# A decoder trunk's compressed-attention branch on one core: four heads in one score bank, one exponent and one sum for all heads, one reduction for the block importance, two heads per transpose

## The chip, the cores and the metric

The kernel runs on one core of one Trainium2 chip. The metric is the device time of one execution in microseconds (us), lower is better. A core has five engines with a queue of instructions each: TensorE (PE in the profile, its weight loads PEld), VectorE (DVE), ScalarE (ACT), GpSimd (POOL) and SyncE (SP, which issues most transfers). TensorE's granted clock is 1.00 when it runs at its upper level of 2.4 GHz.

## The reference, cut to what matters

The trunk has two layers on a stream of 1024 tokens of width 1024, all in float32. Layer A is a sparse attention with 16 heads in 4 groups (4 query heads share one key/value head, head width 64) and three branches: compressed blocks, selected blocks and a sliding window. Layer B is a dilated attention over shared keys. Each layer ends in a gated feed-forward part. Only layer A's compressed branch is changed in what it computes with:

```python
k_cmp = compress(kvh(kc), pe_k, w1_k, w2_k)          # 63 blocks of 32 tokens, stride 16
v_cmp = compress(kvh(vc), pe_v, w1_v, w2_v)          # gelu(blk @ w1) @ w2
s = einsum('bsgrd,bngd->bgrsn', q, k_cmp) * scale
p, denom, _ = masked_softmax(s + bias_c, dist_c >= 0)
p_cmp = p / maximum(denom, 1e-30)
o_cmp = einsum('bgrsn,bngd->bsgrd', p_cmp, v_cmp)
imp = einsum('bgrsn,nj->bgsj', p_cmp, overlap)       # 16 selection blocks, summed over the 4 heads
...                                                  # forced blocks, top 8 of 16 -> mask of the selected branch
o = g[..., 0:1] * o_cmp + g[..., 1:2] * o_sel + g[..., 2:3] * o_win
```

A selection block overlaps five compressed blocks, so its importance is a sum over 5 positions and 4 heads.

## The kernel before, in words

**Stages.** Layer A's projections (0 to about 288 us; `compress` makes the compressed keys `kc` and values `vc` in it), layer A's attention (about 288 to 722 us), the dense rest of layer A with the feed-forward part and the projections for layer B (to about 1905 us), layer B's attention (to about 2235 us), and the dense rest of layer B.

**Layer A's attention** runs over 32 units: 4 groups g times 8 token tiles t of 128 tokens. A unit has one `cmp_job` (compressed branch, 4 heads) and four `dense_job`s (window or selected branch, two heads each). A unit's `cmp_job` is written down between the first two dense jobs of the unit before. Each job makes scores on PE in a bank named `s` (3 of them), adds the bias and takes the row minimum on DVE (scores are kept negated, so the minimum is the softmax's maximum), exponentiates on ACT, and scales on POOL. Its second half (`back`) transposes the probabilities on PE into a bank `pt` (3 of them), splits them into two float32r parts `th` (ACT, line 346) and `tl` (DVE, line 347) and multiplies them with the values into the unit's output bank `o` (2 of them). Each value tile holds its high and low float32r parts side by side (64 + 64 columns), which `evac_o` adds.

**cmp_job before** (lines 810 to 867). nv = min(8t+7, 63) is the number of compressed blocks that a tile can see. Four score matmuls go to two `s` banks (line 817, two PE passes each); four custom DVE instructions add the bias and take the minimum, one for each head (line 825, each with a read of its accumulator); four exponentials with a running sum, one for each head (line 829, ACT, each with a read of its accumulator); `cd` is the sum (lines 831, 832); `dg` is its inverse times the gate (line 836). POOL multiplies (line 840, and 839 for `pn`, which only tiles with t >= 4 need). For t >= 4 the importance comes from a DVE reduction over heads into `a4` (line 844), one over 4 blocks (line 847) and an addition for the fifth (line 848); then force, the 8 largest, and the mask `mk` (849 to 855). The mask is transposed on PE (line 860) and copied by ACT into the extra rows `QM` of the queries (line 861), which the selected branch's score matmuls read (line 896). `back` makes four transposes of 128 x 128 (64 columns of each are zero), the split at 512 columns, and two matmuls of 512 columns (865, 866).

**dense_job before** (lines 869 to 924). Line 895/896 are the score matmuls, 898 the eviction with the minimum, 904 the exponential, 906 the inverse, 908 POOL's scaling, 483 the transposes, 507/508 the value matmuls. For the third key block of the window (t >= 2) the transposed block is first copied out whole (line 499, `tra` by ACT for one pair of heads, `trv` by DVE for the other) and split on POOL (lines 500, 501).

**Order.** Within both attention stages the order of each engine's queue is written out by class `Order`: it lists the instructions, estimates with `hold` how long each occupies its engine, and simulates the queues. An instruction's place among its engine's due ones is its place in the program plus an offset from the table RANK_A or RANK_B, by engine and tile name. The order is then fixed by dependencies; for SP it isn't. Each engine runs its queue strictly in that order.

Of the kernel before, what the change touches and what calls it, by code (L numbers as in the profile page):

```python
# [11 lines left out]
F32 = mybir.dt.float32  # L12
F32R = mybir.dt.float32r
BF = mybir.dt.bfloat16
AF = mybir.ActivationFunctionType
# [10 lines left out]
G = 4  # L26
DH = 64
# [50 lines left out]
class Ring:  # L78
# [14 lines left out]
    ("Activation", "P1"): 5, ("Activation", "QM"): -15, ("Activation", "ot"): 155, ("Activation", "pc"): -20,  # L93
    ("Activation", "th"): -280, ("Activation", "tra"): 10, ("Activation", "twa"): 5, ("DVE", "P1"): 45,
# [7 lines left out]
}  # L102
RANK_B = {
    ("Activation", "P"): 175, ("Activation", "cc"): -385, ("Activation", "crow0"): -375,
    ("Activation", "crow1"): 70, ("Activation", "mrow"): -665, ("Activation", "ot"): 165,
    ("Activation", "th"): -705, ("Activation", "tra"): 40, ("Activation", "twa"): 125, ("DVE", "P"): -95,
    ("DVE", "cc"): -40, ("DVE", "crow0"): 190, ("DVE", "crow1"): -170, ("DVE", "mx"): -345, ("DVE", "o12"): -35,
    ("DVE", "oTb"): 10, ("DVE", "s12"): -45, ("DVE", "tl"): 15, ("DVE", "trv"): -15, ("DVE", "twv"): -105,
    ("PE", "o"): 245, ("PE", "pt"): -40, ("PE", "s"): 25, ("Pool", ""): -655, ("Pool", "T"): -350,
    ("Pool", "oTb"): 380, ("Pool", "thp"): 1255, ("Pool", "tlp"): 30, ("SP", "K"): 95, ("SP", "Q"): 105,  # L110
    ("SP", "T"): 95, ("SP", "V"): -375,
# [3 lines left out]
class Order:  # L115
# [43 lines left out]
    def hold(self, i, e):  # L159
# [5 lines left out]
        if e == "DVE":  # L165
            if sb and not two and i.opcode != "TensorReduce":
                return 90 + 0.63 * n
            return 75 + 1.05 * n + 65 * some + 120 * (sb and n < 64)
        if e == "Activation":
            return 315 + 0.825 * n if len(outs) > 1 else 100 * some + (108 + 0.84 * n if sb else 85 + 0.81 * n)  # L170
        if e == "Pool":
            if not wide:
                return 430 if i.opcode == "RegisterMove" else 120
            if two:
                return 185 + 2.15 * n
            return 200 + 2.5 * n if outs[0].dtype == F32R else 320 + 0.84 * n if n > 64 else 170 + n
# [121 lines left out]
def trunk(ctx, tc, I, out):  # L298
# [24 lines left out]
    def bank(name):  # L323
        return psum[name].tile([128, 512], F32, name=name, bufs=BANKS.get(name, 1))
# [223 lines left out]
    vc = ares.tile([128, G, 128], F32R, name="vc")  # L548
# [4 lines left out]
    with ExitStack() as c:  # L553
# [51 lines left out]
        def compress(i, kc2, weights):  # L605
# [35 lines left out]
            else:  # L641
                for g in range(G):
                    for hd in range(2):
                        nc.tensor.matmul(ps2[0:64, g * 64:(g + 1) * 64], hid[:, hd, g * 64:(g + 1) * 64],
                                         w2t[:, hd, 0, :], start=hd == 0, stop=hd == 1)
                nc.scalar.activation(vc[64:128], kc2[64:128, :, 0:128], AF.Copy, scale=0.0)
                split(vc[0:64, :, 0:64], vc[0:64, :, 64:128], ps2[0:64].rearrange("p (g d) -> p g d", d=64))
# [80 lines left out]
    with ExitStack() as c:  # L728
# [70 lines left out]
        pcs = [wk.tile([128, 4, 128], F32, name=f"pc{i}") for i in range(2)]  # L799
        for pc in pcs:  # L800
            nc.gpsimd.memset(pc[:, :, 64:], 0.0)
# [5 lines left out]
        def query(g, t, hh):  # L807
            return grp["Q", g, t // 4, hh][:, tok(t % 4)]

        def cmp_job(g, t):  # L810
            C = grp["C", g]
            nv = min(8 * t + 7, 63)
            psv = []
            for hp in range(2):
                ps = bank("s")[:].rearrange("p (e n) -> p e n", e=2)
                for e in range(2):
                    nc.tensor.matmul(ps[:, e, :DH], f32(query(g, t, 2 * hp + e)), kc[:, g, :], start=True, stop=True)
                    psv.append(ps[:, e, :])
            pc = pcs[(g * NT + t) % 2]
            pv = pc[:, :, :nv]  # L820
            nc.gpsimd.memset(pc[:, :, nv:64], 0.0)
            mx = wk.tile([128, 4], F32, name="cm", bufs=3)
            dn = wk.tile([128, 4], F32, name="cd", bufs=3)
            for hh in range(4):
                nc.vector.tensor_tensor_reduce(out=pc[:, hh, :nv], in0=psv[hh][:, :nv],
                                               in1=C[:, hh, 56 - 8 * t:56 - 8 * t + nv], scale=1.0, scalar=3e38,
                                               op0=OP.add, op1=OP.min, accum_out=mx[:, hh:hh + 1])
            for hh in range(4):
                nc.scalar.activation(pc[:, hh, :nv], pc[:, hh, :nv], AF.Exp, bias=mx[:, hh:hh + 1], scale=-1.0,
                                     accum_out=dn[:, hh:hh + 1])  # L830
            nc.vector.tensor_scalar(dn, dn, 1e-30, None, op0=OP.max)
# [3 lines left out]
            dg = wk.tile([128, 4], F32, name="dg", bufs=3)  # L835
            nc.vector.tensor_mul(dg, dn, gt(g, t, 0, 0, 4))
            if t >= 4:
                pn = wk.tile([128, 4, 64], F32, name="pn", bufs=1)
                nc.gpsimd.tensor_mul(pn[:, :, :nv], pv, dn[:].unsqueeze(2).to_broadcast([128, 4, nv]))
            nc.gpsimd.tensor_mul(pv, pv, dg[:].unsqueeze(2).to_broadcast([128, 4, nv]))  # L840
            if t >= 4:
                a4 = wk.tile([128, 68], F32, name="a4", bufs=2)
                nc.gpsimd.memset(a4, 0.0)
                nc.vector.tensor_reduce(a4[:, 1:1 + nv], pn[:, :, :nv].rearrange("p h n -> p n h"), axis=AX.X,
                                        op=OP.add)
                sc = wk.tile([128, 16], F32, name="sc", bufs=2)
                nc.vector.tensor_reduce(sc, a4[:, 1:65].rearrange("p (j i) -> p j i", i=4), axis=AX.X, op=OP.add)
                nc.vector.tensor_add(sc, sc, a4[:, 0:64].rearrange("p (j i) -> p j i", i=4)[:, :, 0])
# [6 lines left out]
                nc.vector.tensor_scalar(mk, s2_, -2e38, BIG, op0=OP.is_gt, op1=OP.mult)  # L855

            def back():
# [1033 lines left out]
```

## Time and profile before, and how to read it

| | us |
|---|---|
| median of 3 runs | 3004.94 (2999.41 to 3007.05) |
| the profiled execution's own time | 3006.98 |
| its span | 3005.2 |
| layer A's attention in it | 288 to 722 |
| layer B's attention in it | about 1905 to 2235 |

The profile gives for each engine how long it was busy and what ended the idle time before its instructions. Register, branch and DMA-issuing instructions don't count as busy. Matmuls overlap each other: a row's duration holds the time through the array, so the pace of a run of matmuls is read from the starts of neighbours, not from their durations. A read of an accumulator is an instruction of its own and partly lies beside the next one.

### The profile page before, as it was taken

How to read it: one execution, taken by the hardware profiler on the slowest of the kernel's cores; microseconds unless marked ns; L12 is line 12 of the kernel's file. 1: busy time of each engine (PE TensorE's matmuls, PEld its weight loads, DVE VectorE, ACT ScalarE, POOL GpSimd, SP SyncE). 2: the span in 40 equal slices, each digit the busy share in tenths (PEclk: the TensorE clock that was granted, in tenths of full speed). 3: DMA queues.
4: the chain of work that ended last, by engine and by line, in shares of the span. 5: the costliest groups of instructions: out<-in, count | busy, mean ns of one | idle time of the engine just before them, and what ended most of it. 6: DMA issues, size and time to landing. Idle time of an engine off the chain costs nothing. (4 is left out here: it accounts for less than half of the span.)

```text
span 3005.2 us, 44518 instructions
## 1 busy us (share of the span) xinstructions
PE 2859.3 (95%) x14670; PEld 2376.2 (79%) x14670; DVE 2404.8 (80%) x4832; ACT 1599.1 (53%) x3596; POOL 1641.1 (55%) x1751
## 2 busy tenths in 40 slices
PE   7999999998999999999999999899988899999997
PEld 6988888887777788878777788788866678888886
DVE  5432899998988988988875676699979788888887
ACT  5432898886453333333454444699955433333334
POOL 2134676767666555555556786333348655555551
PEclk9999999999999999999999999999999999999999
DMA  6766033112012232232224555976420212111112
GB/s 170 223 186 177 31 107 86 45 45 106 29 58 66 64 77 67 56 76 62 85 81 132 162 169 156 280 199 174 129 82 25 66 48 62 53 53 56 57 46 74
DMA packets 266839, 294.51 MB, mean 98 GB/s; under 512 B 18099, under 2 KB 209475, under 8 KB 266608
## 3 DMA queue, kind: packets, MB, share of 16 engines
q1 hardware_dynamic: 246960, 231.50, 26.8%
q0 software_dynamic: 19648, 60.16, 6.6%
q8 instruction: 117, 1.92, 0.3%
q14 instruction: 114, 0.93, 0.1%
HBM read 228.49 MB, written 78.81 MB: 102 GB/s over the span
## 5 line engine op out<-in xcount | busy, mean ns | idle before, releaser
L986 DVE TENSOR_TENSOR pl<-oT,ph 128x512 fp32r<-128x512 f32 x315 | 333.8, 1079 | 41.5 <-ACT ph L985 35.8
L985 ACT ACTIVATE ph<-oT 128x512 fp32r<-128x512 f32 x329 | 198.9, 626 | 220.8 <-PE ux L374 61.1
L483 PE MATMUL pt<-ident,P 128*128 128x128 f32 x1536 | 263.4, 279 | 9.8 <-ACT P L1682 4.0
L986 DVE TENSOR_TENSOR pl<-oTb,ph 128x512 fp32r<-128x512 f32 x229 | 221.7, 993 | 24.3 <-ACT ph L985 24.3
L985 ACT ACTIVATE ph<-oTb 128x512 fp32r<-128x512 f32 x239 | 143.3, 626 | 181.8 <-PE ux L374 54.5
L1044 DVE TENSOR_TENSOR xr<-xr,dr 128x512 f32<-128x512 f32 x336 | 214.4, 678 | 28.6 <-PE dr L375 28.6
L1044 DVE TENSOR_TENSOR xr<-xr,dx 128x512 f32<-128x512 f32 x352 | 220.1, 677 | 2.4 <-PE dx L375 1.7
L347 DVE TENSOR_TENSOR tl<-pt,th 128x512 fp32r<-128x512 f32 (+1 forms) x320 | 202.9, 652 | 18.5 <-ACT th L346 17.0
L374 PE MATMUL dx<-pl,ph 128*128 128x512 f32 x512 | 204.8, 402 | 9.3 <-DVE pl L986 8.5
L483 PEld LDWEIGHTS pt<-ident,P 128*128 128x128 f32 x1536 | 182.9, 142 | 37.1 <-ACT P L1682 8.7
L908 POOL TENSOR_SCALAR P<-P,sm,gates 128x384 f32<-128x384 f32 (+7 forms) x256 | 183.8, 729 | 39.1 <-DVE sm L906 36.8
L375 PE MATMUL dx<-ph,pl 128*128 128x512 f32 x512 | 200.6, 396 | 0.2 <-DVE pl L986 0.2
L346 ACT ACTIVATE th<-pt 128x512 fp32r<-128x512 f32 (+1 forms) x320 | 174.9, 566 | 31.1 <-PE pt L483 26.3
L1305 POOL TENSOR_TENSOR oT<-oT,gffn 128x512 f32<-128x512 f32 x92 | 109.8, 1199 | 127.9 <-DMA oT<-in_ffn_w_up_dram 114.2
L904 ACT ACTIVATE P<-P,m 128x384 f32<-128x384 f32 (+7 forms) x256 | 171.1, 671 | 11.9 <-DVE m L902 11.5
L373 PE MATMUL dx<-ph 128*128 128x512 f32 x512 | 158.0, 400 | 7.2 <-ACT ph L985 2.9
L1305 POOL TENSOR_TENSOR oTb<-oTb,gffn 128x512 f32<-128x512 f32 x92 | 109.2, 1196 | 84.2 <-DMA oTb<-in_ffn_w_up_dram 70.0
L1682 ACT ACTIVATE P<-P,st 128x384 f32<-128x384 f32 (+2 forms) x256 | 139.6, 548 | 4.0 <-DVE st L1677 2.8
L507 PE MATMUL o<-th,V 128*128 128x256 f32 x476 | 138.2, 305 | 1.3 <-DVE oTb L520 0.9
L508 PE MATMUL o<-tl,V 128*128 128x256 f32 x476 | 135.0, 301 | 0.1
L1677 DVE CUSTOM_DVE_ANT_0 P<-s,T 128x384 f32<-128x384 f32 (+2 forms) x256 | 114.2, 478 | 20.0 <-PE pt L483 6.9
L374 PEld LDWEIGHTS dx<-pl,ph 128*128 128x128 f32 x512 | 97.7, 191 | 40.8 <-DVE pl L986 21.5
(629 smaller groups left out, 9569.1 us busy)
## 6 DMA issues: line engine op xcount, KB each, us to landing
qB<-xr POOLq DMA_DIRECT2D x96, 256.0 KB, 4.7
oT<-in_ffn_w_up_dram SPq DMA_DIRECT2D x92, 256.0 KB, 3.0
oTb<-in_ffn_w_up_dram SPq DMA_DIRECT2D x92, 256.0 KB, 3.0
Q<-qB SPq DMA_DIRECT2D x40, 512.0 KB, 7.0
wd<-in_ffn_w_down_dram SPq DMA_DIRECT2D x66, 256.0 KB, 2.6
oT<-in_b_w_q_dram SPq DMA_DIRECT2D x48, 256.0 KB, 3.3
K<-kBs SPq DMA_DIRECT2D x40, 256.0 KB, 10.2
wraw<-in_a_w_in_dram SPq DMA_DIRECT2D x18, 512.0 KB, 5.0
```

Source lines behind the costliest of these rows:

```text
L346: nc.scalar.activation(H_, src, AF.Copy)
L347: nc.vector.tensor_sub(L_, src, f32(H_))
L373: nc.tensor.matmul(ps, lh, rh, start=first, stop=False, skip_group_check=bool(shared))
L374: nc.tensor.matmul(ps, lh, rl, start=False, stop=False, skip_group_check=bool(shared))
L375: return nc.tensor.matmul(ps, ll, rh, start=False, stop=last, skip_group_check=bool(shared))
L483: nc.tensor.transpose(ps[:, i * 128:(i + 1) * 128], b, ident)
L904: nc.scalar.activation(P[:, e, :n], P[:, e, :n], AF.Exp, bias=mm[:, e:e + 1], scale=-1.0, accum_out=sm[:, e:e + 1])
L908: nc.gpsimd.tensor_scalar(P[:, e, :n], P[:, e, :n], sm[:, e:e + 1], gt(g, t, br, 2 * hp + e, 1), op0=OP.mult, op1=OP.mult)
L985: nc.scalar.activation(h, src, AF.Copy)
L986: (eng or nc.vector).tensor_sub(l, src, f32(h))
L1044: nc.vector.tensor_add(xs, xs, banks[t])
L1305: nc.gpsimd.tensor_mul(v, v, gains[:, k:k + 4].unsqueeze(2).to_broadcast([128, 4, 128]))
```

## The change

- `cmp_job`: four heads' scores go to one bank. DVE adds the bias for all heads in one instruction and takes the minima in one reduction; POOL subtracts (minimum minus score, the minimum broadcast over the blocks); ACT takes one exponential without a sum; DVE takes the four sums in one reduction. The guard of the sum against zero stays only for t = 0.
- For t >= 4 `pn` becomes a lasting tile of 65 columns a head, with a zero in front; one DVE reduction over a view `near` of 16 blocks x 4 heads x 5 positions gives the importance. The gate is multiplied onto `pn`, not onto `pc` through `dg`. `a4` goes.
- `back`: `pc` has 64 columns a head, two heads go through one transpose, the split has 256 columns, and four matmuls of 256 columns replace two of 512. For that `vc` holds the values twice, once with zeros in the lower and once in the upper 64 rows; `compress` makes the second copy (two more POOL copies, 128 instead of 64 output rows of eight matmul pairs, one more zero fill and one more split).
- The window's third block is copied by ACT for both pairs of heads (`tra`), no longer by DVE for one.
- RANK_A and RANK_B get new numbers throughout, and `hold` new estimates for DVE reductions and POOL products with a broadcast. Layer B's instructions are the same, their order isn't.

```diff
 RANK_A = {
...
+    ("Activation", "P1"): 70, ("Activation", "P2"): 97, ("Activation", "QM"): -712, ("Activation", "ot"): 59,
...
 RANK_B = {
...
+    ("Activation", "P"): 168, ("Activation", "cc"): -1338, ("Activation", "crow0"): -291,
...
         if e == "DVE":
-            if sb and not two and i.opcode != "TensorReduce":
+            if i.opcode == "TensorReduce":
+                return 5 + 2.08 * n
+            if sb and not two:
                 return 90 + 0.63 * n
...
             if two:
-                return 185 + 2.15 * n
+                return 185 + (1.66 if any(a.ap[-1][0] == 0 for a in wide) else 2.15) * n
...
-    vc = ares.tile([128, G, 128], F32R, name="vc")
+    vc = ares.tile([128, 2, G, 128], F32R, name="vc")
...
+                both = cp.tile([128, 2, G, 2, 64], F32, name="both")
+                for e in range(2):
+                    nc.gpsimd.tensor_copy(both[:, :, :, e, :], hid[:].rearrange("p h (g n) -> p h g n", n=64))
                 for g in range(G):
                     for hd in range(2):
-                        nc.tensor.matmul(ps2[0:64, g * 64:(g + 1) * 64], hid[:, hd, g * 64:(g + 1) * 64],
+                        nc.tensor.matmul(ps2[:, g * 64:(g + 1) * 64], both[:, hd, g].rearrange("p e n -> p (e n)"),
                                          w2t[:, hd, 0, :], start=hd == 0, stop=hd == 1)
-                nc.scalar.activation(vc[64:128], kc2[64:128, :, 0:128], AF.Copy, scale=0.0)
-                split(vc[0:64, :, 0:64], vc[0:64, :, 64:128], ps2[0:64].rearrange("p (g d) -> p g d", d=64))
+                for e in range(2):
+                    own, oth = slice(64 * e, 64 * e + 64), slice(64 - 64 * e, 128 - 64 * e)
+                    nc.scalar.activation(vc[oth, e], kc2[oth, :, 0:128], AF.Copy, scale=0.0)
+                    split(vc[own, e, :, 0:64], vc[own, e, :, 64:128], ps2[own].rearrange("p (g d) -> p g d", d=64))
...
-        pcs = [wk.tile([128, 4, 128], F32, name=f"pc{i}") for i in range(2)]
...
+        pcs = [wk.tile([128, 4, 64], F32, name=f"pc{i}") for i in range(2)]
+        pn = wk.tile([128, 4, 65], F32, name="pn")
+        nc.gpsimd.memset(pn[:, :, 0:1], 0.0)
+        step = pn[:].ap
+        near = bass.AP(tensor=pn[:].tensor, offset=pn[:].offset, ap=[step[0], [4, 16], [65, 4], [1, 5]])
...
-            for hp in range(2):
-                ps = bank("s")[:].rearrange("p (e n) -> p e n", e=2)
...
+            ps = bank("s")[:, :256].rearrange("p (h n) -> p h n", n=64)
+            for hh in range(4):
+                nc.tensor.matmul(ps[:, hh, :], f32(query(g, t, hh)), kc[:, g, :], start=True, stop=True)
...
-            for hh in range(4):
-                nc.vector.tensor_tensor_reduce(out=pc[:, hh, :nv], in0=psv[hh][:, :nv],
...
-            for hh in range(4):
-                nc.scalar.activation(pc[:, hh, :nv], pc[:, hh, :nv], AF.Exp, bias=mx[:, hh:hh + 1], scale=-1.0,
-                                     accum_out=dn[:, hh:hh + 1])
-            nc.vector.tensor_scalar(dn, dn, 1e-30, None, op0=OP.max)
+            nc.vector.tensor_add(pv, ps[:, :, :nv], C[:, :, 56 - 8 * t:56 - 8 * t + nv])
+            nc.vector.tensor_reduce(mx, pv, axis=AX.X, op=OP.min)
+            nc.gpsimd.tensor_sub(pv, wide_(mx[:], nv), pv)
+            nc.scalar.activation(pv, pv, AF.Exp)
+            nc.vector.tensor_reduce(dn, pv, axis=AX.X, op=OP.add)
+            if t == 0:
+                nc.vector.tensor_scalar(dn, dn, 1e-30, None, op0=OP.max)
             nc.vector.reciprocal(dn, dn)
...
-            dg = wk.tile([128, 4], F32, name="dg", bufs=3)
-            nc.vector.tensor_mul(dg, dn, gt(g, t, 0, 0, 4))
             if t >= 4:
-                pn = wk.tile([128, 4, 64], F32, name="pn", bufs=1)
-                nc.gpsimd.tensor_mul(pn[:, :, :nv], pv, dn[:].unsqueeze(2).to_broadcast([128, 4, nv]))
-            nc.gpsimd.tensor_mul(pv, pv, dg[:].unsqueeze(2).to_broadcast([128, 4, nv]))
-            if t >= 4:
-                a4 = wk.tile([128, 68], F32, name="a4", bufs=2)
-                nc.gpsimd.memset(a4, 0.0)
-                nc.vector.tensor_reduce(a4[:, 1:1 + nv], pn[:, :, :nv].rearrange("p h n -> p n h"), axis=AX.X,
-                                        op=OP.add)
+                nc.gpsimd.tensor_mul(pn[:, :, 1:], pc, wide_(dn[:], 64))
+                nc.gpsimd.tensor_mul(pc, pn[:, :, 1:], wide_(gt(g, t, 0, 0, 4), 64))
                 sc = wk.tile([128, 16], F32, name="sc", bufs=2)
-                nc.vector.tensor_reduce(sc, a4[:, 1:65].rearrange("p (j i) -> p j i", i=4), axis=AX.X, op=OP.add)
-                nc.vector.tensor_add(sc, sc, a4[:, 0:64].rearrange("p (j i) -> p j i", i=4)[:, :, 0])
+                nc.vector.tensor_reduce(sc, near, axis=AX.XY, op=OP.add)
...
+            else:
+                dg = wk.tile([128, 4], F32, name="dg", bufs=3)
+                nc.vector.tensor_mul(dg, dn, gt(g, t, 0, 0, 4))
+                nc.gpsimd.tensor_mul(pv, pv, wide_(dg[:], nv))
...
-                th, tl = transposed(wk, [pc[:, hh, :] for hh in range(4)])
+                th, tl = transposed(wk, [pc[:, 2 * hp:2 * hp + 2, :].rearrange("p e n -> p (e n)") for hp in range(2)])
                 po = po_[g, t] = bank("o")
-                nc.tensor.matmul(po, vc[:, g, :], th, start=True, stop=False, skip_group_check=True)
-                nc.tensor.matmul(po, vc[:, g, :], tl, start=False, stop=False, skip_group_check=True)
+                for e in range(2):
+                    o_ = po[:].rearrange("p (c e q) -> p c e q", e=2, q=128)[:, :, e, :]
+                    for i, x in enumerate((th, tl)):
+                        nc.tensor.matmul(o_, vc[:, e, g, :], x[:, :256].rearrange("p (c q) -> p c q", q=128),
+                                         start=e == i == 0, stop=False, skip_group_check=True)
...
                     th, tl = transposed(wk, [P[:, e, b * 128:(b + 1) * 128] for b in bs for e in range(2)],
-                                        (cp_a, cp_v)[hp] if br == 2 and b0 == 2 else None, 1 if br == 2 and b0 == 2 else 4,
+                                        cp_a if br == 2 and b0 == 2 else None, 1 if br == 2 and b0 == 2 else 4,
```

## Rows read from the trace of the kernel before

**Rows 1.** The busy time of each engine in stretches of the span (us from its start): length, then for PE, PEld, DVE, ACT and POOL the busy us and the number of instructions, then the granted clock, the DMA share and GB/s.

```profile
200.00:220.00 20.00, 20.00 (x105) 16.29 (x104) 4.76 (x6) 4.61 (x8) 7.58 (x16) 1.00 0.84 266
288.00:722.00 434.00, 412.64 (x2875) 366.80 (x2874) 395.03 (x1590) 379.04 (x1122) 297.33 (x487) 1.00 0.22 62
1920.00:2220.00 300.00, 282.98 (x2031) 250.98 (x2030) 262.97 (x862) 259.90 (x771) 83.97 (x145) 0.97 0.57 162
```

**Rows 2.** Starts of neighbouring matmuls on PE, from the instructions in order of time: start us, duration us, engine, line, operation, tiles, shape, how many merged.

```profile
283.69 0.39 PE L374 MATMUL mm<-hL,wh 128*128 128x512 f32 x1
283.92 0.39 PE L375 MATMUL mm<-hH,wl 128*128 128x512 f32 x1
...
470.55 1.15 PE L483 MATMUL pt<-ident,P 128*128 128x128 f32 x9
...
474.43 0.28 PE L508 MATMUL o<-tl,V 128*128 128x256 f32 x1
...
474.55 0.28 PE L507 MATMUL o<-th,V 128*128 128x256 f32 x1
```

**Rows 3.** Who waited for whom in layer A's attention, all engines: waiting engine, tile and line, the releaser, us in total, times, longest us.

```profile
DVE P L898 <- PE s L896: 10.7, 31, 0.9
PE pt L860 <- DVE mk L855: 7.8, 14, 0.8
PEld s L895 <- DVE mp L898: 4.2, 11, 0.7
PEld pt L483 <- POOL P L908: 4.0, 13, 0.5
PEld s L895 <- DVE m L898: 4.0, 15, 0.5
```

**Rows 4.** Groups of DVE instructions in layer A's attention, some with their shapes apart: line, operation, tiles, shapes, count, busy us and mean ns of one, idle us before them and what ended it.

```profile
L825 DVE CUSTOM_DVE_ANT_0 pc<-s,C 128x7 f32<-128x7 f32 (+7 forms) x128 | 19.6, 189 | 3.6 <-PE s L817 1.4 <-PE pt L483 0.9 <-POOL P L908 0.2
L825 DVE DVE_READ_ACCUMULATOR2_ANT cm<- 128x1 f32 x128 | 10.5, 82 | 0.0
...
L347 DVE TENSOR_TENSOR tl<-pt,th 128x512 fp32r<-128x512 f32 x183 | 122.0, 685 | 7.4 <-ACT th L346 6.3
L347 DVE TENSOR_TENSOR tl<-pt,th 128x256 fp32r<-128x256 f32 x36 | 15.0, 416 | 1.5 <-ACT th L346 1.5
...
L844 DVE TENSOR_REDUCE a<-pn 128x63 f32<-128x252 f32 x4 | 2.4, 610 | 0.0
L844 DVE TENSOR_REDUCE a<-pn 128x39 f32<-128x156 f32 x4 | 1.7, 430 | 0.0
L847 DVE TENSOR_REDUCE sc<-a 128x16 f32<-128x64 f32 x16 | 3.4, 213 | 0.1
```

**Rows 5.** The other DVE groups of layer A's attention that the change removes, in whole or in part, columns as in rows 4.

```profile
L844 DVE TENSOR_REDUCE a<-pn 128x39 f32<-128x156 f32 (+3 forms) x16 | 8.3, 518 | 0.5 <-POOL pn L839 0.5
L848 DVE TENSOR_TENSOR sc<-sc,a 128x16 f32<-128x16 f32 x16 | 3.8, 239 | 0.4
L836 DVE TENSOR_TENSOR dg<-cd,gates 128x4 f32<-128x4 f32 x32 | 7.8, 245 | 0.9
L831 DVE TENSOR_SCALAR cd<-cd 128x4 f32<-128x4 f32 x32 | 6.1, 189 | 0.5 <-ACT pc L829 0.4
L499 DVE COPY trv<-pt 128x256 f32<-128x256 f32 x24 | 10.1, 420 | 0.3 <-PE pt L483 0.3
```

**Rows 6.** Groups of ACT instructions in layer A's attention, columns as in rows 4.

```profile
L829 ACT ACTIVATE pc<-pc,cm 128x7 f32<-128x7 f32 (+7 forms) x128 | 40.0, 316 | 0.1
L829 ACT ACTIVATION_READ_ACCUMULATOR pc<-pc,cm 128x1 f32 x128 | 24.7, 193 | 0.0
...
L829 ACT ACTIVATE pc<-pc,cm 128x63 f32<-128x63 f32 x16 | 5.5, 348 | 0.0
L829 ACT ACTIVATE pc<-pc,cm 128x7 f32<-128x7 f32 x16 | 4.6, 292 | 0.0
...
L346 ACT ACTIVATE th<-pt 128x512 fp32r<-128x512 f32 x183 | 105.0, 593 | 16.3 <-PE pt L483 13.3 <-PE o L507 0.6 <-ACT P L904 0.5
L346 ACT ACTIVATE th<-pt 128x256 fp32r<-128x256 f32 x36 | 13.7, 379 | 1.4 <-PE pt L483 0.9 <-PE o L507 0.4
L499 ACT COPY tra<-pt 128x256 f32<-128x256 f32 x24 | 8.9, 369 | 0.3 <-PE pt L483 0.3
```

**Rows 7.** Groups of POOL instructions in layer A's attention, columns as in rows 4, and one run of POOL's scalings from the instructions in order of time.

```profile
L840 POOL TENSOR_TENSOR pc<-pc,dg 128x28 f32<-128x28 f32 (+7 forms) x32 | 13.5, 422 | 19.2 <-DVE dg L836 7.8 <-ACT th L346 5.9 <-ACT P L904 2.3
L839 POOL TENSOR_TENSOR pn<-pc,cd 128x156 f32<-128x156 f32 (+3 forms) x16 | 8.5, 528 | 27.4 <-DVE cd L832 16.1 <-ACT th L346 11.3
L843 POOL MEMSET a<- 128x68 f32 x16 | 2.4, 157 | 2.4 <-PE mm L375 1.5 <-DVE sc L848 0.9
L908 POOL TENSOR_SCALAR P<-P,sm,gates 128x512 f32<-128x512 f32 x16 | 12.2, 773 | 4.3 <-DVE sm L906 4.3
...
469.22 4.40 POOL L908 TENSOR_SCALAR P<-P,sm,gates 128x768 f32<-128x768 f32 x5
```

**Rows 8.** The end of the values' compression, from the instructions in order of time, columns as in rows 2.

```profile
205.12 0.38 ACT L628 ACTIVATE hid<-cmp 128x256 f32<-128x256 f32 x1
...
208.67 0.33 PE L644 MATMUL cmp<-w2t,hid 128*64 128x64 f32 x2
...
209.82 1.03 PE L644 MATMUL cmp<-w2t,hid 128*64 128x64 f32 x14
```

More of the change, by code (lines that the diff above doesn't have):

```diff
@@ L92 @@
 RANK_A = {
-    ("Activation", "P1"): 5, ("Activation", "QM"): -15, ("Activation", "ot"): 155, ("Activation", "pc"): -20,
-    ("Activation", "th"): -280, ("Activation", "tra"): 10, ("Activation", "twa"): 5, ("DVE", "P1"): 45,
[7 rows of a table removed]
+    ("Activation", "P1"): 70, ("Activation", "P2"): 97, ("Activation", "QM"): -712, ("Activation", "ot"): 59,
+    ("Activation", "pc"): -105, ("Activation", "th"): -684, ("Activation", "twa"): -1006, ("DVE", "P1"): 170,
[4 rows of a table added]
+    ("Pool", "TW"): 139, ("Pool", "pc"): -615, ("Pool", "pn"): -101, ("Pool", "thp"): -2008,
+    ("Pool", "tlp"): -998, ("SP", "K"): -261, ("SP", "KD"): -1002, ("SP", "KW"): -415, ("SP", "Q"): 2990,
+    ("SP", "QM"): 224, ("SP", "T"): -553, ("SP", "V"): 296, ("SP", "VW"): -274,
 }
 RANK_B = {
[L104 to L111, printed above, removed]
+    ("Activation", "P"): 168, ("Activation", "cc"): -1338, ("Activation", "crow0"): -291,
+    ("Activation", "crow1"): 203, ("Activation", "mrow"): -26, ("Activation", "ot"): 238,
+    ("Activation", "th"): -1633, ("Activation", "tra"): -76, ("Activation", "twa"): -292, ("DVE", "P"): -162,
+    ("DVE", "cc"): -395, ("DVE", "crow0"): 53, ("DVE", "crow1"): 998, ("DVE", "mx"): 185, ("DVE", "o12"): -153,
+    ("DVE", "oTb"): -92, ("DVE", "s12"): 1240, ("DVE", "tl"): -50, ("DVE", "trv"): -3497, ("DVE", "twv"): -34,
+    ("PE", "o"): 347, ("PE", "pt"): -671, ("PE", "s"): 142, ("Pool", ""): -1997, ("Pool", "T"): 1430,
+    ("Pool", "oTb"): -489, ("Pool", "thp"): 2306, ("Pool", "tlp"): -665, ("SP", "K"): 47, ("SP", "Q"): 73,
+    ("SP", "T"): 61, ("SP", "V"): 83,
 }
@@ L797, in load_v @@
             nc.sync.dma_start(f32(t_), vS[i, 4 * a:4 * a + 4, :, g, :].rearrange("t p d -> p t d"))
-        pcs = [wk.tile([128, 4, 128], F32, name=f"pc{i}") for i in range(2)]
-        for pc in pcs:
-            nc.gpsimd.memset(pc[:, :, 64:], 0.0)
+        pcs = [wk.tile([128, 4, 64], F32, name=f"pc{i}") for i in range(2)]
[3 more added lines that the diff above has]
+        near = bass.AP(tensor=pn[:].tensor, offset=pn[:].offset, ap=[step[0], [4, 16], [65, 4], [1, 5]])
         units = [(g, t) for g in range(G) for t in range(NT)]
@@ L812, in cmp_job @@
             nv = min(8 * t + 7, 63)
-            psv = []
-            for hp in range(2):
-                ps = bank("s")[:].rearrange("p (e n) -> p e n", e=2)
-                for e in range(2):
-                    nc.tensor.matmul(ps[:, e, :DH], f32(query(g, t, 2 * hp + e)), kc[:, g, :], start=True, stop=True)
-                    psv.append(ps[:, e, :])
+            ps = bank("s")[:, :256].rearrange("p (h n) -> p h n", n=64)
+            for hh in range(4):
+                nc.tensor.matmul(ps[:, hh, :], f32(query(g, t, hh)), kc[:, g, :], start=True, stop=True)
             pc = pcs[(g * NT + t) % 2]
             pv = pc[:, :, :nv]
-            nc.gpsimd.memset(pc[:, :, nv:64], 0.0)
+            wide_ = lambda x, n: x.unsqueeze(2).to_broadcast([128, 4, n])
+            nc.gpsimd.memset(pc[:, :, nv:], 0.0)
             mx = wk.tile([128, 4], F32, name="cm", bufs=3)
             dn = wk.tile([128, 4], F32, name="cd", bufs=3)
-            for hh in range(4):
-                nc.vector.tensor_tensor_reduce(out=pc[:, hh, :nv], in0=psv[hh][:, :nv],
-                                               in1=C[:, hh, 56 - 8 * t:56 - 8 * t + nv], scale=1.0, scalar=3e38,
-                                               op0=OP.add, op1=OP.min, accum_out=mx[:, hh:hh + 1])
-            for hh in range(4):
-                nc.scalar.activation(pc[:, hh, :nv], pc[:, hh, :nv], AF.Exp, bias=mx[:, hh:hh + 1], scale=-1.0,
-                                     accum_out=dn[:, hh:hh + 1])
-            nc.vector.tensor_scalar(dn, dn, 1e-30, None, op0=OP.max)
+            nc.vector.tensor_add(pv, ps[:, :, :nv], C[:, :, 56 - 8 * t:56 - 8 * t + nv])
[5 more added lines that the diff above has]
+                nc.vector.tensor_scalar(dn, dn, 1e-30, None, op0=OP.max)
             nc.vector.reciprocal(dn, dn)
```

11 rows, old and new, of the table RANK_A are left out of this document.

## The prediction

> **What bounds the kernel now.** I read the busy time by stretches first. All that the change touches lies in layer A's attention, 434 us long, apart from the values' compression before it and the order of layer B's attention. In those 434 us PE is busy 412.6 us, DVE 395.0, ACT 379.0, POOL 297.3, at a granted clock of 1.00 throughout [rows 1]. So no transfer and no clock limits the stage (DMA share 0.22); three engines stand between 87% and 95%. PE's figure is less full than it looks: a row's duration holds the way through the array. Neighbours start 0.23 us apart at 512 columns, 0.12 at 256, and nine transposes in a row take 1.15 us, (1.15 - 0.28) / 8 = 0.11 each [rows 2], while their durations are 0.39 and 0.28. DVE's durations have no such slack, except reads of accumulators, so I take DVE, with 39 us idle, as the engine nearest its limit. The waits bear this out: PE's named waits are nearly all for DVE (the mask `mk` 7.8 us; score banks not yet evicted, 4.2 and 4.0 us on the weight loads), DVE's largest is 10.7 us for scores [rows 3]. What takes work off DVE should shorten the stage, until PE's own pace or a wait takes over.
>
> **DVE, part by part.** A unit has on average 4 x 35 = 140 scores per partition.
> - *Gone.* The four evictions: 19.6 us and 32 last accumulator reads at 0.08, 2.6, so 22.2 (30.1 if no read lay beside another instruction) [rows 4]. `a4` 8.3, the reduction over it 3.4, the addition 3.8, half of `dg` 3.9, 28 of 32 guards 5.3, `trv` 10.1 [rows 4, 5]. The `tl` split shrinks from 512 to 256 columns: 32 x (0.685 - 0.416) = 8.6 [rows 4]. Sum 65.6.
> - *New.* The bias addition reads PSUM and SBUF like `tl`: from its two shapes 0.147 us + 1.05 ns per column, at 140 0.294 us. The reductions: the rows at 64, 156 and 252 elements (213, 430, 610 ns) lie near one line, 78 ns + 2.11 ns per element [rows 4]. At 140 that is 0.373 us, twice a unit; at 320 (the importance, 16 units) 0.753 us. Sum 32 x (0.294 + 0.746) + 16 x 0.753 = 45.3.
> - *Net* -20.3 us of 395.0.
>
> Here a rule speaks otherwise. The reductions' rows cost about 2.1 ns for each further element [rows 4]. The Trainium skill, page "VectorE: DVE Perf Modes", section "The perf-mode tier table", gives `tensor_reduce` one element per cycle, which with the page's 0.96 GHz would be an estimated 1.04 ns. The measured line decides; what half its slope would give is a rival below.
>
> **ACT.** Gone: 40.0 us and 32 last reads at 0.19, 46.2 [rows 6]. New: one exponential without a read; the rows at 7 and 63 columns extend to 0.425 us at 140, an upper end since they carry the sum; the `th` copy's line gives 0.28. I take 0.35, 11.2 us. `th` at 256 columns saves 32 x (0.593 - 0.379) = 6.8; 24 more window copies add 24 x 0.369 = 8.9 [rows 6]. Net -32.9: ACT stops being close to a limit. Both copies now share the one tile `tra`, so the second waits until POOL has split the first; exponentials and `th` queue behind it on ACT. The two are a whole job apart; the 32.9 us freed cover it.
>
> **PE.** 64 transposes fewer: -7.0 us. Four matmuls of 256 columns instead of two of 512: 32 x (4 x 0.12 - 2 x 0.23) = +0.6 [rows 2]. The score matmuls stay. One `s` bank per unit instead of two makes the 8.2 us of bank waits [rows 3] rarer; I count nothing for it.
>
> **POOL.** The subtraction has the sizes of line 840: +13.5 us. The products at full width: 32 x (0.61 - 0.53) = +2.6. `a4`'s zero fill: -2.4 [rows 7]. Net +13.7 on 297.3, 72% of the stage: hidden, POOL still waits for others.
>
> **The new waits.** DVE's reduction for the sums waits for ACT's exponential, that for POOL's subtraction, that for DVE's minima. Behind the reduction on DVE stand score evictions, for which PE's banks wait; behind the subtraction on POOL stand scalings, for which the transposes wait (4.0 us now [rows 3]). The order puts other work in between: a unit's compressed job is issued one unit, 434 / 32 = 13.6 us, ahead of its use. Nothing, unless POOL is late (second rival).
>
> **The compression of the values.** Two POOL copies of 512 columns, at the price of a scaling of 512 (0.77 us each), stand between the gelu's end (205.5) and the matmuls (208.7) [rows 7, 8]. PE meanwhile runs projections (20.0 of 20.0 us busy) [rows 1], and could run on later too: 0; without that cover 1.5 us plus a place behind POOL's store issues, at most 3. Wider weights in 16 matmuls, from 1.03 / 14 = 0.07 to at most 0.11: +0.6 us on PE [rows 2, 8]. Extra zero fill and split: ACT and DVE are busy under 5 of those 20 us [rows 1], so 0.
>
> **The order tables.** No row shows what another order costs. It can win at most what the fullest engine idles, PE's 434.0 - 412.6 = 21.4 us in layer A and 300.0 - 283.0 = 17.0 in layer B [rows 1]; I take as much for the loss. The instructions of layer B are unchanged, so I take 0 for both and keep 11 us either way for the range. SP's queue is not reordered and no transfer is added.
>
> **The sum.** DVE gives up 20.3 us, PE 7.0 - 0.6 - 0.6 = 5.8, ACT 32.9. The stage should gain between PE's 6 and DVE's 20; since DVE is nearest its limit and its neighbours are relieved as well, three quarters of DVE's: 15 us. The profiled execution took 3006.98 us (span 3005.2), 2.0 above the median of 3004.94. 3006.98 - 15 = 2992 for its like; from the median 2990.
>
> **The rivals.** A measurement of this kernel tells about 0.3%, 9 us, from no change: faster means below 2996, slower above 3014.
> - *PE sets the pace.* Its record of 95% is taken at its word; the queues stay coupled, and only PE's 5.8 us come back: 2999. For it: PE idles least of all [rows 1]. Against: the starts in rows 2.
> - *The mask is late* (slower). The mask's chain gets a POOL step and a reduction more, and POOL runs scalings in rows of up to five, 4.40 us [rows 7]. The mask's transpose already holds PE 14 times for 0.56 us [rows 3]. If POOL's turn comes late, each of the 16 masked units could hold PE 1.5 us more: 16 x 1.5 = 24, less 15: +9, 3014. It eats the whole gain from 15 / 16 = 0.94 us a unit on. Against: 13.6 us of lead.
> - *Layer B's order.* 11 us lost there leaves -4, 3001; its full 17 lost beside a gain of only PE's 6 makes +11, 3016, slower; 11 won gives 2979. Layer B's fullest engine idles more, per us, than layer A's: there is room both ways [rows 1].
> - *Reductions at half the slope.* With 1.05 ns per element, the new ones cost 32 x 2 x 140 x 1.06 ns + 16 x 320 x 1.06 ns = 14.9 us less, DVE gives up 35, three quarters of it is 26: 2979. For it: `a4` is read with large strides, the new scores are not. Against: the row at 64 elements has no stride and lies on the line [rows 4]. (It is the rate that the Trainium skill's page "VectorE: DVE Perf Modes", section "The perf-mode tier table", states, as said above.)
>
> **How the numbers follow.** Forecast 0.60, of it 0.58 below 2996 and 0.02 within the bound; PE's pace 0.14; mask late 0.09; layer B loses 0.08 (0.05 within, 0.03 slower), wins 0.04; half slope 0.05. Faster 0.58 + 0.04 + 0.05 = 0.67, same 0.02 + 0.14 + 0.05 = 0.21, slower 0.09 + 0.03 = 0.12. The range: downwards DVE's full 20 and layer B's 11, 2974; upwards past PE's pace (2999) and a loss in layer B (3001) to 3006, short of the late mask.
>
> **What would show it.** After: layer A's attention near 419 us, DVE busy near 375 in it, ACT near 346, POOL near 311; the reductions at 0.37 us for 140 and 0.75 for 320 elements; line 860's counterpart waiting no more than 0.6 us a time; layer B's stage within a few us of its length. I am wrong if DVE falls by 20 and the stage by less than 6 (PE or the order sets the pace), if the wait for the mask grows past 0.9 us a unit, or if the gain lies in layer B.

## The result, and the profile after

| | before | after |
|---|---|---|
| median | 3005.99 us (2999.41 to 3008.91, 4 runs) | 2970.49 us (2965.65 to 2971.42, 4 runs) |
| ratio after to before | | 0.9882 (95% interval 0.9862 to 0.9902) |
| span of the profiled execution | 3005.2 | 2969.6 |
| layer A's attention | 441.9 | 409.3 |
| layer B's attention | 282.1 | 278.6 |

35.5 us faster, where 15 were forecast; below the range's lower end of 2974. Here and below, layer A's attention runs from the first compressed score on PE to the first `ph` of the output projection on ACT, layer B's from its first wide score on PE to the first `ph` on `oTb`; these marks are sharper than the round ends in rows 1. The spans' 35.6 us are 32.6 in layer A's attention, 3.5 in layer B's, 1.2 and 0.9 in the dense parts, less 2.6 because the stage began later (289.5 against 286.9 us). That start wandered between 286.7 and 289.7 over all kernels below, with and without the second copy of the values, so it is not the change's. Each stage length is read from one profiled execution. Layer B's, with the same instructions and the same table in twelve of the kernels below, lies between 278.0 and 281.7 us, so a few us between two kernels say nothing by themselves.

Busy time of the engines in layer A's attention, columns as in rows 1. First the kernel before, at the sharper marks:

```profile
286.90:728.80 441.90, 419.60 (x2929) 373.10 (x2927) 399.07 (x1596) 383.55 (x1131) 302.58 (x493) 1.00 0.23 63
```

and after:

```profile
289.50:698.80 409.30, 401.84 (x2929) 369.97 (x2927) 372.50 (x1335) 353.50 (x930) 315.60 (x509) 1.00 0.24 68
```

DVE gave up 26.6 us, ACT 30.1, PE 17.8 by its record (whose length depends on what stands next to it), POOL took 13.0. PE idles 7.5 us where it idled 22.3.

The compressed branch's new DVE groups (answering to rows 4 and 5), columns as there, forms together:

```profile
L832 DVE TENSOR_REDUCE cm<-pc 128x4 f32<-128x28 f32 (+7 forms) x32 | 9.6, 299 | 1.1
L831 DVE TENSOR_TENSOR pc<-s,C 128x28 f32<-128x28 f32 (+7 forms) x32 | 9.4, 295 | 0.4
L835 DVE TENSOR_REDUCE cd<-pc 128x4 f32<-128x28 f32 (+7 forms) x32 | 9.4, 292 | 0.9 <-ACT pc L834 0.8
L845 DVE TENSOR_REDUCE sc<-pn 128x16 f32<-128x320 f32 x16 | 7.6, 478 | 0.2
```

and two of the forms by themselves:

```profile
L832 DVE TENSOR_REDUCE cm<-pc 128x4 f32<-128x252 f32 x4 | 1.7, 416 | 0.1
...
L832 DVE TENSOR_REDUCE cm<-pc 128x4 f32<-128x60 f32 x4 | 0.9, 216 | 0.1
```

The addition costs the 0.294 us that was estimated. The reductions don't lie on the line of rows 4: (416 - 216) / 192 = 1.04 ns per element on 153 ns, which at 320 gives 486 for the 478 measured.

The new group of ACT after, columns as in rows 6:

```profile
L834 ACT ACTIVATE pc<-pc 128x28 f32<-128x28 f32 (+7 forms) x32 | 10.0, 313 | 0.2
```

and of POOL, columns as in rows 7:

```profile
L833 POOL TENSOR_TENSOR pc<-cm,pc 128x28 f32<-128x28 f32 (+7 forms) x32 | 13.5, 423 | 5.3 <-DVE cm L832 5.2
L842 POOL TENSOR_TENSOR pn<-pc,cd 128x256 f32<-128x256 f32 x16 | 9.8, 614 | 0.6
```

The exponential comes near its estimate (11.2 us), the subtraction meets it (13.5 us). The largest waits of PE and DVE after, columns as in rows 3:

```profile
DVE tl L349 <- ACT th L348: 9.5, 22, 1.0
DVE P L902 <- PE s L900: 7.9, 17, 0.7
...
PE s L899 <- DVE mp L902: 2.7, 3, 0.9
...
PE pt L485 <- DVE tl L349: 1.3, 1, 1.3
...
PE s L899 <- DVE m L902: 0.9, 2, 0.6
```

The wait of the mask's transpose, 7.8 us in 14 times [rows 3], is down to 0.2 us, as its group shows (PE's groups after, columns as in rows 4):

```profile
L861 PE MATMUL pt<-ident,mk 128*16 128x128 f32 x16 | 4.4, 273 | 0.3 <-DVE mk L852 0.2
```

### The profile page after: what moved, and what is told of

Its sections match the earlier page's. It is cut to its first block, busy times and chain, and to the rows that moved or that the text cites. A ratio compares the mean times of both kernels' runs of the same rounds, so it can differ in the third digit from the quotient of the medians.

```text
span 2969.6 us, 43895 instructions
## 1 busy us (share of the span) xinstructions
PE 2835.3 (95%) x14670; PEld 2367.3 (80%) x14670; DVE 2378.8 (80%) x4573; ACT 1569.7 (53%) x3398; POOL 1657.9 (56%) x1768
## 3 DMA queue, kind: packets, MB, share of 16 engines
q1 hardware_dynamic: 246960, 231.50, 26.7%
## 5 line engine op out<-in xcount | busy, mean ns | idle before, releaser
L349 DVE TENSOR_TENSOR tl<-pt,th 128x512 fp32r<-128x512 f32 (+1 forms) x320 | 194.1, 624 | 24.9 <-ACT th L348 23.2
L348 ACT ACTIVATE th<-pt 128x512 fp32r<-128x512 f32 (+1 forms) x320 | 168.7, 546 | 42.1 <-PE pt L485 27.0
L376 PE MATMUL dr<-pl,ph 128*128 128x512 f32 x288 | 114.9, 399 | 10.5 <-DVE pl L990 10.4
```

Source lines behind the costliest of these rows:

```text
L348: nc.scalar.activation(H_, src, AF.Copy)
L349: nc.vector.tensor_sub(L_, src, f32(H_))
L376: nc.tensor.matmul(ps, lh, rl, start=False, stop=False, skip_group_check=bool(shared))
```

## The experiments

**Work or order?** Four kernels cross the two works (compressed branch and window copy of before or after) with the order's tables.

```diff
 # new_work_old_order: the changed kernel with RANK_A, RANK_B and hold() of before
 # old_work_new_order: the kernel before with RANK_A, RANK_B and hold() of after
 # old_work_no_table, new_work_no_table: RANK_B of before, hold() of after, and
+RANK_A = {}
```

> The changed kernel with both order tables and the order's cost estimates of before: the new work in an order that was chosen for the old work. Theory W (the removed work makes the gain): layer A's attention (first compressed score on PE to the first `ph` on ACT) stays within 8 us of the changed kernel's 409 us, total 2972 to 2980. Rival O (the new order makes about half of it): layer A's attention about 425 us, layer B's back at its old length (+3 us), total about 2988 to 2992.

> The kernel before with both order tables and the cost estimates of the changed kernel. W: layer A's attention near its 442 us or longer (the tables name other tiles), only layer B's 3 us come, total 3000 to 3010. O: layer A's attention about 425 us, total about 2986 to 2990.

> The kernel before with an empty order table for layer A (layer B's table of before) and the changed kernel's cost estimates, for comparison with the next run: neither work has an order tuned for it. W: both are longer than with their tables by about as much, this one 3005 to 3030. O: this one is near 3006.

> The changed kernel with an empty order table for layer A, layer B's table of before, and its own cost estimates. W: 25 to 35 us below the run before this one, all of it in layer A's attention. O: only 10 to 18 us below it.

Measured, with all the later tables (us; A and B are the attention stages in the trace):

| work | layer A's table | A | B | total, ratio to before (95%) |
|---|---|---|---|---|
| old | before's | 441.9 | 282.1 | 1 |
| old | after's | 452.5 | 279.7 | 1.0020 (1.0003 to 1.0037) |
| old | none | 475.4 | 282.6 | 1.0094 (1.0075 to 1.0112) |
| old | own, first | 436.3 | 279.1 | 0.9987 (0.9978 to 0.9997) |
| old | own, second | 436.1 | 280.0 | 0.9931 (0.9915 to 0.9948) |
| new | before's | 433.7 | 282.6 | 0.9954 (0.9938 to 0.9971) |
| new | after's | 409.3 | 278.6 | 0.9882 (0.9862 to 0.9902) |
| new | none | 469.2 | 283.9 | 1.0072 (1.0052 to 1.0092) |
| new | own | 411.4 | 278.4 | 0.9879 (0.9863 to 0.9895) |

Neither theory held throughout: W fell with the new work in the old order (433.7 us, not within 8 of 409), O with the old work in the new one (452.5 us, not 425). The new work in the old order is worth 8.2 us, without any table 6.2, though DVE and ACT give up their time all the same. The new table, with its cost estimates, takes 24.4 us more from the new work and costs the old work 10.6. These figures are rough by the granted clock: it was 1.00 before, after and for the old work without a table, but 0.99 for the new work in the old order and for the old work in the new one (1% of the stage, 4 to 5 us), and 0.98 for the new work without a table (9 us). So the new work in the old order may be worth 12, and the table 20. Nor is the new table made for the old work: it has no entry for `a4` and `trv`, which only the old work has. The new work in the old order, first its busy time:

```profile
287.00:720.70 433.70, 415.20 (x2929) 370.64 (x2927) 375.88 (x1336) 354.42 (x931) 315.09 (x509) 0.99 0.23 64
```

the old work in the new order, and the new work without a table:

```profile
289.70:742.20 452.50, 426.31 (x2929) 377.43 (x2927) 400.28 (x1596) 385.91 (x1131) 301.91 (x493) 0.99 0.22 61
288.20:757.40 469.20, 436.46 (x2929) 379.67 (x2927) 375.76 (x1336) 353.40 (x931) 315.51 (x509) 0.98 0.22 59
```

then the waits of the new work in the old order:

```profile
DVE tl L347 <- ACT th L346: 17.7, 23, 2.1
DVE P L900 <- PE s L898: 11.8, 24, 1.3
...
DVE oT L520 <- ACT ot L518: 7.8, 9, 1.5
PE pt L859 <- DVE mk L850: 5.2, 10, 0.7
...
PE s L897 <- DVE m L900: 3.3, 6, 1.8
```

The first and the third of these in the kernel before (the second, 10.7 us, stands in rows 3):

```profile
DVE tl L347 <- ACT th L346: 9.3, 24, 1.1
...
DVE oT L520 <- ACT ot L518: 2.4, 3, 1.5
```

DVE is nearly as little busy as after, 376 us, but idles 57.8 where it idled 42.8 before: most of the freed time turned into waits for `th` (17.7 for 9.3 us), scores (11.8 for 10.7) and `ot` (7.8 for 2.4), and the mask still holds PE (5.2 us). With the new table these are 9.5, 7.9, 0.2 and 0.2 us. Which of the table's entries does it, no run shows.

**Is the table's gain the work's?** The same random search over the order's own estimates was given to both works, each time with the changed kernel's `hold()` and layer B table; only RANK_A differs. The edit is a table of numbers.

> The kernel before with the changed kernel's cost estimates, the changed kernel's table for layer B, and a table for layer A that a random search over the order's own estimates found for the old work (the sum of its estimates falls from 422 to 403 us; the changed kernel's stands at 390). Theory S (the order's share has nothing to do with the compressed branch): layer A's attention falls from 442 to about 423 us, total about 2985. Rival J (the new order pays only together with the new work): layer A's attention stays at 435 us or above, total 2996 or above.

> The changed kernel with a table for layer A found by the same search with the same start (the table of before) and budget as the old work's own table (estimates 407 to 388 us). Theory J (the work makes room that a searched order can use): layer A's attention 405 to 415 us, so at equal search the changed work is worth 20 us or more against the old work's 436. Rival T (the changed kernel's table is a lucky one, found in another way): layer A's attention 420 us or more.

> The kernel before with the changed kernel's cost estimates and layer B table, and a second table for layer A from the same search, started from the changed kernel's table (estimates 418 to 407 us). J: layer A's attention 430 us or more, as with the first such table (436). T: 425 us or less, since the old work can be ordered as well and the first table was an unlucky one.

The old work got to 436.3 and 436.1 us, the new one, from the table of before, to 411.4, close to the 409.3 of the changed kernel's own. So S fell, and T with it: the two searches gave the old work 5.8 us at most, and at equal search the new work is worth 25 in layer A's attention. By the totals' ratios it is 16 to 32 us, since the other stages vary too. A better table for the old work, found by measuring instead of by the estimates, is not excluded. The estimates can't stand for a run: they promised the old work a fall of 19 us (422 to 403) where 5.6 came, and measured, its two searched tables lie 33 and 29 us above them, the new work's (the changed kernel's own at 390, the searched one at 388) 19 and 23. The same search started from the changed kernel's own table (estimate 387 us) gave an order in which queues wait for each other without end, so there is no time for it.

**Which engine's time counts?** Load was added to one engine at a time, with the order of all other instructions of the stage kept.

```diff
+            # after_plus_dve, before_plus_dve: behind the minima
+            nc.vector.tensor_reduce(jk[:, 4 * x:4 * x + 4], gates[:, 0:4, 0:35], axis=AX.X, op=OP.min)   # x3
+            # after_plus_act: behind the exponential
+            nc.scalar.copy(jk[:, :, 0:35], gates[:, 0:4, 0:35])                      # x3
+            # after_plus_pe, before_plus_pe: behind the fourth score (before: to ps[:, 1, :DH])
+            nc.tensor.matmul(ps[:, 3, :], f32(query(g, t, 3)), kc[:, g, :], start=True, stop=True)   # x4
+            # before_plus_act_small: behind the fourth exponential
+            nc.scalar.copy(jk, gates[:, 0, 0:16])                                    # x6
```

> The changed kernel with three more DVE reductions of 140 elements (to 4 outputs, unused) behind each unit's minima, about 0.9 us a unit, 28 us in all; the order of everything else in layer A's attention is kept. Theory D (DVE's time sets the pace of the stage): layer A's attention grows from 409 us by 22 us or more. Rival P (PE sets it): by less than 12.

> The changed kernel with three more ACT copies of 140 elements behind each unit's exponential, about 0.7 us a unit, 22 us in all; order kept. D and P both: layer A's attention grows by less than 10 us, since ACT is the least loaded of the three. If it grows by 15 or more, every added instruction costs its full time because the queues are coupled in a fixed order, and no single engine is the bound (rival C).

> The changed kernel with the fourth head's score matmul repeated four times a unit (eight PE passes of 0.11 us, 28 us in all); order kept. P: layer A's attention grows by 22 us or more. D: by less than 12.

> The kernel before with the same three DVE reductions a unit, 28 us in all, behind the fourth head's minimum; order kept. D: layer A's attention grows from 442 by 22 us or more, so what DVE gave up in the change was worth its full time. P: by less than 12.

> The kernel before with the fourth head's score matmul repeated four times a unit, 28 us of PE in all; order kept. Slack in the old order: layer A's attention grows by less than 20 us, where the changed kernel's grew by 25.6. No slack: by 25 or more.

> The kernel before with six more ACT copies of 16 elements behind each unit's fourth exponential, some 0.8 us a unit, 25 us of ACT in all; order kept. ACT, the least loaded of the three before: layer A's attention should grow from 442 by less than half of the time that ACT's busy time grows by. If by 0.75 of it or more, ACT's time was as dear before as in the changed kernel, and the four exponentials that went were worth much more than nothing.

ACT's load on the kernel before is of smaller copies, because the larger tile finds no room in SBUF there.

Busy time in layer A's attention, columns as in rows 1. The changed kernel with load on DVE:

```profile
289.30:710.30 421.00, 409.26 (x2929) 370.64 (x2927) 387.57 (x1431) 354.23 (x930) 315.21 (x509) 1.00 0.24 66
```

The changed kernel with load on ACT:

```profile
288.50:714.80 426.30, 410.61 (x2929) 370.00 (x2927) 374.72 (x1335) 375.39 (x1027) 314.92 (x509) 1.00 0.24 65
```

The changed kernel with load on PE:

```profile
287.90:722.80 434.90, 428.51 (x3185) 397.95 (x3184) 373.34 (x1336) 355.11 (x931) 316.45 (x509) 1.00 0.24 64
```

The kernel before with load on DVE:

```profile
288.70:738.00 449.30, 423.92 (x2929) 373.55 (x2928) 414.67 (x1692) 383.91 (x1131) 301.61 (x493) 1.00 0.22 62
```

The kernel before with load on ACT:

```profile
288.00:764.60 476.60, 434.54 (x2929) 381.20 (x2927) 402.26 (x1595) 416.43 (x1322) 301.91 (x493) 0.98 0.21 58
```

The kernel before with load on PE:

```profile
287.90:755.50 467.60, 446.41 (x3185) 402.07 (x3183) 400.13 (x1595) 384.64 (x1130) 301.66 (x493) 1.00 0.22 60
```

| | load added (us of busy time) | stage grew | per us |
|---|---|---|---|
| after, DVE | 15.1 | 11.7 | 0.77 |
| after, ACT | 21.9 | 17.0 | 0.78 |
| after, PE | 26.7 | 25.6 | 0.96 |
| before, DVE | 15.6 | 7.4 | 0.47 |
| before, ACT | 32.9 | 34.7 | 1.05 |
| before, PE | 26.8 | 25.7 | 0.96 |

Busy time is not all that a load takes. One load on DVE in the changed kernel, and DVE's next instruction, from the instructions in order of time (columns as in rows 2):

```profile
291.51 0.70 DVE L842 TENSOR_REDUCE jk<-gates 128x4 f32<-128x140 f32 x3
292.13 0.28 DVE L912 CUSTOM_DVE_ANT_0 P<-s,TW 128x128 f32<-128x128 f32 x1
```

The reductions last 0.289 us each but start (0.70 - 0.29) / 2 = 0.205 apart, and the next instruction starts 0.62 after the first: neighbours' records overlap. So the load holds DVE's queue for 19.7 us in 32 units (0.615 each at the median), where the busy time grew by 15.1. Counted like this, from a load's first start to the next instruction's, the loads are 19.7 us on DVE, 28.4 on ACT and 28 on PE after (256 passes of 0.11), and 19.9, 41.0 and 28 before. A us then costs 0.59, 0.60 and 0.91 after, and 0.37, 0.85 and 0.92 before. In the run of the kernel before with load on ACT the granted clock was 0.98: if it lengthened the whole stage by its 2%, 9.5 us, ACT's price before is 0.77 by busy time and 0.61 by this count.

No theory comes out whole. D falls by PE's 25.6 us and ACT's 17.0. P's mark is met on PE, but it too has ACT's load under 10 us. C's 15 us on ACT are reached, but not "its full time": no engine of the three is free, a us on PE costs nearly all of itself in either order, on ACT more than half, on DVE a third to three fifths. The two loads on DVE came out smaller than the 28 us that their marks of 22 and 12 us were made for, so 11.7 and 7.4 decide nothing between D and P by themselves. In the kernel before PE met the mark for no slack (25.7 us for 25) and ACT the 0.75 (1.05, or 0.77), and ACT, 87% busy, was dearer than DVE at 90% by either count. What this can't tell apart: the loads stand in the compressed branch, and PE's, written to a bank that the eviction then waits for, lengthen its chain as well as fill an engine.

**Which part of the work?** One part undone at a time in the changed kernel, each with a table from the same search.

```diff
 # without_pairing: four transposes, pc of 128 columns a head, one vc, two matmuls of 512, as before
 # without_importance
-                nc.vector.tensor_reduce(sc, near, axis=AX.XY, op=OP.add)
+                nc.vector.tensor_reduce(a4[:, 1:65], pn[:, :, 1:].rearrange("p h n -> p n h"), axis=AX.X, op=OP.add)
+                ...
 # without_one_exponent: four tensor_tensor_reduce and four Exp with accum_out, as before; no tensor_sub
 # without_copy
-                                        cp_a if br == 2 and b0 == 2 else None, ...
+                                        (cp_a, cp_v)[hp] if br == 2 and b0 == 2 else None, ...
```

> The changed kernel without the pairing of heads in transposes (four transposes, 512 columns split, one copy of the values in `vc`), with a table for layer A of its own from the same search (estimates 396 us, against 388 for the whole change). Theory D (DVE's time alone counts): DVE gets 8.6 us back, layer A's attention about 419 us against 411. Rival C (every engine's time counts): PE's 6, ACT's 7 and DVE's 9 us come back together, 420 us or more.

> The changed kernel with the importance by `a4` again (two reductions and an addition; the first reads 64 elements apart), table of its own (estimates 389 us). D and C: DVE gets about 8 us back, layer A's attention about 418 us. If it stays within 3 us of 411, this part brought nothing.

> The changed kernel with four evictions and four exponentials with their sums per unit again, in one score bank, without POOL's subtraction; table of its own (estimates 397 us). ACT gets some 35 us back, POOL loses 13, DVE loses about 6. D: layer A's attention 411 us or less. C: 420 us or more.

> The changed kernel with the window's third block copied by DVE for one pair of heads again, table of its own (estimates 393 us): 10 us move from ACT to DVE. D: layer A's attention about 421 us. C: the sum over the engines hardly changes, 414 us or less.

| undone | A | against 411.4 | DVE busy | ACT busy | total, ratio to before (95%) |
|---|---|---|---|---|---|
| (nothing, searched table) | 411.4 | | 373.6 | 352.4 | 0.9879 (0.9863 to 0.9895) |
| pairing | 426.4 | +15.0 | 381.5 | 359.7 | 0.9917 (0.9897 to 0.9938) |
| importance | 414.0 | +2.6 | 382.3 | 354.1 | 0.9883 (0.9866 to 0.9901) |
| one exponent, one sum | 427.1 | +15.7 | 365.0 | 383.7 | 0.9940 (0.9922 to 0.9958) |
| window copy on ACT | 423.9 | +12.5 | 381.9 | 346.9 | 0.9918 (0.9900 to 0.9937) |

The telling one is the exponent, whose busy times (columns as in rows 1) against the searched table's are DVE 8.6 us shorter, ACT 31 longer, and the stage 15.7 longer:

```profile
286.90:714.00 427.10, 411.64 (x2929) 372.31 (x2927) 365.02 (x1495) 383.70 (x1154) 303.00 (x477) 1.00 0.24 65
```

D falls here. The importance gives DVE the same 8.6 us back and costs next to nothing, where both theories said 418 us. The window copy fits D better than C: 8.2 us more on DVE, 5.5 fewer on ACT, 12.5 longer. So no theory fits all four. The order's own estimates, 8, 1, 9 and 5 us above the 388 of the whole change, ranked them right, at about half of their size. The four add up to 45.8 us, not 25: they aren't additive, and each table is one find of a search; two searched tables for one work differed by 0.2 us (old), a searched one and the changed kernel's own by 2.1 (new).

**The reduction's price.** In the kernel before, heads of a block side by side:

```diff
-                pn = wk.tile([128, 4, 64], F32, name="pn", bufs=1)
+                pn = wk.tile([128, 64, 4], F32, name="pn", bufs=1)
...
-                nc.vector.tensor_reduce(a4[:, 1:1 + nv], pn[:, :, :nv].rearrange("p h n -> p n h"), axis=AX.X,
+                nc.vector.tensor_reduce(a4[:, 1:1 + nv], pn[:, :nv, :], axis=AX.X,
```

> The kernel before, with `pn` stored with the four heads of a block next to each other, so that the reduction over heads (before: 610 ns for 252 elements, read 64 elements apart) reads neighbours; POOL's product writes with gaps instead. If the step between elements was what made it slow: near 140 ns + 1.07 ns per element, 410 ns at 252. If a reduction to 63 outputs of 4 is slow by itself: 600 ns still. The total is not the question.

DVE's groups in that run, columns as in rows 4:

```profile
L844 DVE TENSOR_REDUCE a<-pn 128x63 f32<-128x252 f32 x4 | 1.6, 411 | 0.1
...
L844 DVE TENSOR_REDUCE a<-pn 128x39 f32<-128x156 f32 x4 | 1.2, 304 | 0.0
```

252 elements in 411 ns instead of 610 [rows 4], as expected: the step between elements was the price. POOL's product at 252 went from 608 to 663 ns. DVE was 2.9 us less busy (396.2), with the same order; the stage took 441.7 us, 0.2 less.

## Why the prediction was wrong, point by point

- **The order tables, taken as 0: the step that failed.** Of layer A's 32.6 us, 24.4 come only with the new table (20 if the clock of 0.99 cost its 1%), beyond the 11 us kept for the range and about the 21.4 that PE idled. Nor was that a limit. From the old order to the new, the new work's idle time on PE falls from 18.5 to 7.5 us and PE's record from 415.2 to 401.8: the record itself shrinks by 13.4 us, part of it perhaps by the clock. The prediction had found that record longer than the work in it [rows 2], and then took what it leaves idle for the most that an order can win. The order is also not a term of its own: at equal search the work is worth 25 us, in the old order 8. Layer B's table gave its share alone: 279.4 us on the mean of the twelve kernels with it, 282.9 on the mean of the eight without, 3.5 us, inside the 11.
- **DVE as the one engine, ACT's 33 us and PE's 6 counted as nothing: failed too.** Busy shares of 95, 91 and 87% in a coupled fixed order don't name one bound: before, a us of busy time added to ACT cost 0.77 to 1.05, to PE 0.96, to DVE 0.47, and undoing the one exponent costs 15.7 us against DVE's saving. That DVE's durations have no slack but in reads of accumulators is wrong: the reductions added to the changed kernel last 0.289 us each and start 0.205 apart. "Three quarters of DVE's" had no row behind it.
- **The reductions, mis-sized.** 35.9 us were forecast, 26.6 measured; DVE's net was -26.6, not -20.3. The line in rows 4 joined a reduction with neighbouring elements (64 elements, 213 ns, on both lines) to ones read 64 elements apart. The rival of the half slope had the slope right and blamed the stride, but left the fixed part at 78 ns for 153 measured (its reductions come to 21.0 us); that its 2979 comes near the measured time is luck, since the time came with the order and the other engines. The Trainium skill, page "VectorE: DVE Perf Modes", section "The perf-mode tier table", gives `tensor_reduce` the 1x mode, which by the page is one element per cycle, an estimated 1.04 ns at its 0.96 GHz. The packed rows agree (1.04 ns), the strided ones don't ((610 - 430) / 96 = 1.9 ns [rows 4]). But the importance, whose reduction was the most over-priced (0.753 us for 0.478), is worth 2.6 us.
- **ACT -32.9, POOL +13.7 as busy time: right** (-30.1, +13.0), and POOL stayed hidden: the exponential behind its subtraction waited 0.2 us in all.
- **The values' compression, 0: right.** POOL's two copies took 0.61 and 1.39 us; the stage's start doesn't follow them.
- **The late mask: the other way.** Its wait went from 7.8 to 0.2 us, with the new table; in the old order it was still 5.2 us.
- **PE's pace, a rival**: 2999 is far off, but 28 us more on PE cost 25.6 after and 25.7 before, though PE idled 22.3 us then and 7.5 now: PE's time was nearly full price in both. Whether PE alone would hold the stage now, no run tells.

## What to carry to other kernels

Where several engines stand near 90% in a hand-written order, don't choose one: price what is taken off each of them, by the starts of neighbours and not by durations, and treat a new order as part of the change, since here most of the work taken away in the old order turned into waits. An added load on one engine with the order kept shows in one run what that engine's time is worth. Price an instruction from a row with the same step between its elements.

## What the runs showed of the hardware

- A DVE reduction of 252 float32 took 610 ns read 64 elements apart, 411 side by side; a POOL product of 252 took 663 ns writing with gaps, 608 without.
- Three independent DVE reductions of 140 elements in a row, 289 ns each by their record, started 205 ns apart: neighbours overlap.
